# Two of the modulation's sums move from TensorE to VectorE in a two-layer diffusion backbone

## Chip, core and metric

The kernel runs on one core of one Trainium2 chip. The metric is device time in microseconds (us) of one execution. The engines are called PE (TensorE, matmuls), DVE (VectorE), ACT (ScalarE), POOL (GpSimd) and SP (SyncE); SP and POOL here issue the DMAs.

## What is computed

Two layers of a network over 256 latent tokens and 256 context tokens, 1024 wide. In each layer a modulation vector is made from the conditioning `c` (for latents) and `c_ctx` (for context), six pieces of 1024: shift, scale and gate for the mixer, then the same for the feed-forward part (FFN).

```python
mod = jax.nn.silu(c) @ w_mod[l] + b_mod[l]            # w_mod[l]: 1024 x 6144
mod_c = jax.nn.silu(c_ctx) @ w_mod[l] + b_mod[l]
sh1, sc1, g1, sh2, sc2, g2 = jnp.split(mod[:, None, :], 6, axis=-1)
shc1, scc1, gc1, shc2, scc2, gc2 = jnp.split(mod_c, 6, axis=-1)
h = rmsnorm(x, g_pre_mix[l]) * (1 + sc1) + sh1
hc = rmsnorm(xc, g_pre_mix[l]) * (1 + scc1) + shc1
y, y_ctx = token_mixer(h, hc, lp, row, col, ctx_out)   # attention, mLSTM, window attention, Fourier
x = x + g1 * rmsnorm(y, g_post_mix[l])
h2 = rmsnorm(x, g_pre_ffn[l]) * (1 + sc2) + sh2
x = x + g2 * rmsnorm(conv_ffn(h2, ...), g_post_ffn[l])
# the context stream goes the same way in the first layer
```

## The kernel before

All activations lie feature-major: 8 tiles of 128 features by 512 tokens (`KT` = 8, `T` = 512; tokens 0 to 255 are context, 256 to 511 latent; the two halves are called segments 0 and 1 below). Every large product is three matmuls (L232 to L234): weights and activations are split into a high and a low part, weights by ACT (L212) and DVE (L213), activations by ACT (`hh`) and DVE (`hl`).

The modulation is computed in rounds. `mod_rounds` takes a list of rounds, six for a layer; each round is 1024 of the 6144 outputs and reads `w_mod` in 8 pieces of 128 x 1024 (k = 0 to 7), 512 KB each. A round that is not in its argument `vector` adds up over k on PE: four matmuls for each k (L647), each with 32 columns of stationary `cs` (only two are not zero: silu of `c` and of `c_ctx`) and 256 moving columns. A round in `vector` adds up over k on DVE into two tiles of 128 x 1024, one for `c` and one for `c_ctx`: L634 for k = 0, L636 for the others, with the conditioning value as a scalar for each partition. At the end eight matmuls with a column of ones add over the partitions (L642). Both ways end with a transpose on DVE and a few small operations.

The pieces and the two sums are tiles of the pool `u`, which has 16 buffers and also holds, among much else, the four tiles of the residual stream `x` and the high and low parts of the weights loaded ahead for the FFN's first products. A round goes forward one k at a time where `between` or `fill` calls it. In layer 0 the rounds 2, 3, 4 go forward during the mixer, with loads on POOL's queue; layer 1's rounds 0, 1, 3 go forward in layer 0's `channel` (output projection, then FFN) as a filler of PE's waiting times, with loads on SP's queue.

PE's order and, in `channel`, SP's order are those of the program text (`manual_schedule`). DVE, ACT and POOL are ordered by a scheduler that works from its own costs when the program is built and takes the buffers of the pools too; on the chip each engine then keeps that order.

The place that matters besides the mixer is the closing of layer 0's projection. `closing` and `post_end` make the sums for the norm (L436 on PE, then a chain of small DVE operations), and for each of the 8 feature tiles m and each segment the residual (L522, L527), the normed tile (L401), `hh` and a full copy on ACT (L404, L408) and `hl` on DVE (L410) are made. The finished `x` tiles are written to memory by POOL (L561), two feature tiles at a time. PE's next work, the FFN's first four products, needs them m by m: first all of segment 0, then all of segment 1 (96 matmuls of 256 columns each):

```python
if j == 0:
    self.first = [[self.pf([T]) for _ in w] for w in self.ahead]
    for cs in segs:
        steps = [self.gemm_steps(p[:, cs], w, h, cs) for ps, ws in zip(self.first, self.ahead) for p, w in zip(ps, ws)]
        for _ in zip(*steps, strict=True):
            pass
```

Of the kernel before, what the change touches and what calls it, by code (L numbers as in the profile page):

```python
# [153 lines left out]
class Net:  # L154
# [1278 lines left out]
    def run(self):  # L1433
        nc = self.nc
        self.start()
        self.queue, self.fillers, self.owed, self.mods = [], [], 0, {}
        part = self.squares(self.x, slice(0, T))
        ps = self.pa([T])
        for i, p in enumerate(part):
            nc.tensor.matmul(ps, self.one, p, start=i == 0, stop=i == len(part) - 1)  # L1440
        nc.vector.tensor_scalar(self.xms, self.fold(ps, T), 1.0 / D, EPS, op0=ALU.mult, op1=ALU.add)
        rb = self.t2([T], tag="rs")
        self.unfold(self.rsqrt(self.xms), rb)
        h = self.new_h()
        A = None
        self.wtm = []
        mod, load = self.mod_rounds(0, (0, 1), nc.sync, parts=2)
        for _ in range(KT):
            load()
        after = ((), (7,), (3, 7), (3, 7, 7))  # L1450
        for q in range(4):
            self.wtm += [self.tm_weights(0, i, i >= 3) for i in ((0,), (1,), (2,), (3, 4))[q]]
            for k in range(KT):
                next(mod)
                for _ in range(after[q].count(k)):
                    next(self.tm_steps)
            ms = (2 * q, 2 * q + 2)
            A, B = self.gain(0, 1, V_GPRE, True, "A1", ms, A), self.shift(0, 0)
            for m in range(*ms):
                self.modulate(h, m, self.streams(0), rb, A, B, True)  # L1460
            if q == 0:
                self.tm_start(h, NT)
        self.start2()
        mod, load = self.mod_rounds(0, (2, 3, 4), nc.gpsimd, (3,))
        self.queue = [mod]
        for l in range(L):
            last = l == L - 1
            c0 = CTX if last else 0
            if self.dbg:
                for k in range(KT):  # L1470
                    self.dbg(f"hh{l}_{k}", h[k][0].bitcast(F32))
            if last:
                mod, load = self.mod_rounds(1, (4,), nc.gpsimd)
                self.queue = [mod]
            later, self.load = self.mod_rounds(1, (5,) if last else (0, 1, 3), nc.sync, () if last else (1, 3))
            al = self.mixer(l, h, c0)
            while self.queue:
                self.between()
            self.fillers = [later]
            if not last:  # L1480
                self.fillers.append(self.mod_rounds(0, (5,), nc.sync, (5,))[0])
            with self.tc.manual_schedule(engines={mybir.EngineType.SP}):
                h = self.channel(l, al, c0, self.load)
# [88 lines left out]
```

## Time and profile before

| | |
|---|---|
| median of three runs | 1450.48 us (1449.2 to 1450.76) |
| the profiled execution: its time, its span | 1452.06 us, 1450.3 us |
| PE busy | 1394.2 us (96%) |
| DVE busy | 957.4 us (66%) |
| ACT busy | 663.6 us (46%) |
| mean granted clock of PE | 0.987 of full |

The span runs from the first to the last instruction; 1.76 us of the execution's time lie around it. Matmuls overlap, so a matmul's own duration is longer than the step from one start to the next; costs on PE are read from starts.

### The profile page before, as it was taken

Reading aid. Unit: us, or ns where it says so; the run is one execution under the profiler, and the core shown is the slowest. Engines: PE = TensorE matmul, PEld = TensorE weight load, DVE = VectorE, ACT = ScalarE, POOL = GpSimd, SP = SyncE. Lnnn points to the kernel's source line nnn. Section 1 sums busy time; section 2 is a strip of 40 time slices with the busy share of each in tenths; the row PEclk is TensorE's granted clock in tenths of the full one; section 3 lists DMA queues with packets and bytes.
Section 4 is the critical chain, followed back from the end, with each engine's and each line's share of the span. In section 5 each row is a group of like instructions: output and inputs, shape, how many; then the busy total and the mean of one; then the engine's idle time right before and its main releaser. Section 6 shows DMA issues by size and latency. Waiting matters only on the chain.

```text
span 1450.3 us, 22235 instructions
## 1 busy us (share of the span) xinstructions
PE 1394.2 (96%) x8657; PEld 1177.2 (81%) x8657; DVE 957.4 (66%) x1955; ACT 663.6 (46%) x1156; POOL 36.3 (3%) x69
## 2 busy tenths in 40 slices
PE   6999999999999999999999999899999999899996
PEld 3887777777778889878888888687989898799996
DVE  5448687746653788853554667958676877765666
ACT  3436434324432655422332336656553655455454
POOL 0000000100000000000000000100000000000000
PEclk8999999999999999999999999999999999999998
DMA  9722232343223634343335432562333467357663
GB/s 289 272 83 92 88 132 87 131 160 102 59 73 97 206 134 168 137 160 116 116 118 163 145 117 90 202 217 88 117 115 118 136 188 244 117 174 224 184 183 94
DMA packets 73417, 208.00 MB, mean 143 GB/s; under 512 B 6880, under 2 KB 24672, under 8 KB 73184
## 3 DMA queue, kind: packets, MB, share of 16 engines
q1 hardware_dynamic: 65792, 179.32, 39.0%
q0 software_dynamic: 7520, 27.27, 5.4%
q8 instruction: 68, 1.11, 0.3%
q14 instruction: 37, 0.30, 0.1%
HBM read 201.31 MB, written 5.24 MB: 142 GB/s over the span
## 4 chain that ended last, share of the span: by engine, by line
PE 74%; DVE 8%; ACT 2%; DMA 2%; issue 1%; DVEq 0%; ACTq 0%
PE pg L232 16%; PE pg L233 15%; PE pg L234 15%; PE pa L233 7%; PE pa L232 7%; PE pa L234 7%; PE pa L787 2%; DVE wl L213 1%; PE pa L817 1%; PE pa L856 1%; PE pa L840 1%; ACT wh L212 1%; PE pa L1176 1%; PE pa L647 1%; DMA u<-wmod 1%
## 5 line engine op out<-in xcount | busy, mean ns | idle before, releaser
L213 DVE TENSOR_TENSOR wl<-st,wh 128x1024 fp32r<-128x1024 f32 (+2 forms) x262 | 313.9, 1203 | 214.9 <-ACT wh L212 213.4
L212 ACT CAST wh<-st 128x1024 fp32r<-128x1024 f32 (+2 forms) x262 | 268.8, 1032 | 370.0 <-PE pg L233 202.6
L232 PE MATMUL pg<-hh,wh 128*128 128x512 f32 (+1 forms) x1136 | 403.9, 356 | 0.7 <-DVE tg L1266 0.7
L234 PE MATMUL pg<-hh,wl 128*128 128x512 f32 (+1 forms) x1136 | 385.2, 339 | 2.3 <-DVE wl L213 2.3
L233 PE MATMUL pg<-hl,wh 128*128 128x512 f32 (+1 forms) x1136 | 384.4, 338 | 0.0
L232 PEld LDWEIGHTS pg<-hh,wh 128*128 128x128 f32 x1136 | 216.8, 191 | 31.1 <-issue 5.7
L234 PEld LDWEIGHTS pg<-hh,wl 128*128 128x128 f32 x1136 | 216.7, 191 | 26.7 <-DVE wl L213 3.1
L233 PEld LDWEIGHTS pg<-hl,wh 128*128 128x128 f32 x1136 | 216.9, 191 | 23.3 <-issue 3.1
L232 PE MATMUL pa<-hh,wh 128*128 128x256 f32 (+1 forms) x376 | 126.0, 335 | 1.4 <-ACT hh L288 1.4
L233 PE MATMUL pa<-hl,wh 128*128 128x256 f32 (+1 forms) x376 | 126.1, 335 | 0.1
L234 PE MATMUL pa<-hh,wl 128*128 128x256 f32 (+1 forms) x376 | 125.9, 335 | 0.0
L232 PE MATMUL pg<-u,wh 128*128 128x256 f32 (+1 forms) x350 | 119.8, 342 | 0.0
L233 PE MATMUL pg<-u,wh 128*128 128x256 f32 (+1 forms) x350 | 115.0, 329 | 0.0
L234 PE MATMUL pg<-u,wl 128*128 128x256 f32 (+1 forms) x350 | 114.8, 328 | 0.0
L232 PEld LDWEIGHTS pa<-hh,wh 128*128 128x128 f32 x376 | 71.4, 190 | 8.7 <-ACT hh L288 1.6
L233 PEld LDWEIGHTS pa<-hl,wh 128*128 128x128 f32 x376 | 71.4, 190 | 7.7 <-DVE hl L289 0.6
L234 PEld LDWEIGHTS pa<-hh,wl 128*128 128x128 f32 x376 | 71.4, 190 | 7.1
L232 PEld LDWEIGHTS pg<-u,wh 128*128 128x128 f32 x350 | 65.9, 188 | 12.1 <-issue 5.9
L234 PEld LDWEIGHTS pg<-u,wl 128*128 128x128 f32 x350 | 65.8, 188 | 6.6
L233 PEld LDWEIGHTS pg<-u,wh 128*128 128x128 f32 x350 | 65.9, 188 | 6.3 <-issue 0.7
L636 DVE SCALAR_TENSOR_TENSOR u<-u,cs,u 128x1024 f32<-128x1024 f32 x49 | 61.6, 1279 | 2.0 <-DMA u<-wmod 1.9
L828 ACT ACTIVATE pp<-pa,nbias 128x512 f32<-128x512 f32 (+1 forms) x48 | 29.5, 615 | 68.0 <-DVE nbias L826 37.2
(296 smaller groups left out, 2137.8 us busy)
## 6 DMA issues: line engine op xcount, KB each, us to landing
st<-wup SPq DMA_DIRECT2D x88, 512.0 KB, 3.7
st<-wgate SPq DMA_DIRECT2D x64, 512.0 KB, 3.6
u<-wmod SPq DMA_DIRECT2D x48, 512.0 KB, 4.9
u<-wmod POOLq DMA_DIRECT2D x32, 512.0 KB, 5.1
st<-wdn SPq DMA_DIRECT2D x32, 448.0 KB, 3.3
st<-win SPq DMA_DIRECT2D x26, 512.0 KB, 3.7
u<-wmod SPq DMA_DIRECT2D x32, 256.0 KB, 6.1
st<-wbr SPq DMA_DIRECT2D x16, 512.0 KB, 3.7
```

The lines of the kernel that those rows point to most:

```text
L212: nc.scalar.copy(hi[:, :cols], st[:, :cols])
L213: nc.vector.tensor_tensor(lo[:, :cols], st[:, :cols], hi.bitcast(F32)[:, :cols], op=ALU.subtract)
L232: mm(out, ah, bh, start=i == 0, stop=False)
L233: mm(out, ah, bl, start=False, stop=False)
L234: mm(out, al, bh, start=False, stop=i == n - 1)
L636: nc.vector.scalar_tensor_tensor(t, st, self.cs[:, k, i:i + 1], t, op0=ALU.mult, op1=ALU.add)
L647: nc.tensor.matmul(ps[32 * g:32 * g + 32], self.cs[:, k], st[:, g], start=k == 0, stop=k == KT - 1)
L787: ins = self.nc.tensor.matmul(O[:, j], lhs[i], rhs[i], start=i == 0, stop=i == n - 1)
L817: nc.tensor.matmul(S[:, :n], q, k, start=i == 0, stop=i == len(ops) - 1 and not m)
L828: nc.scalar.activation(P[:, :n], S[:, :n], AF.Exp, bias=nb, scale=scale, accum_out=den)
L840: nc.tensor.transpose(S[:, j * 128:j * 128 + 128], P[:, j * 128:j * 128 + 128], self.ident)
L856: ins = nc.tensor.matmul(O[64 * i:64 * i + 64, f], v_of(j, 2 * f + i), PT[i][:, j * 128:j * 128 + 128], start=j == 0, stop=j == n // 128 - 1)
```

## The change

Round 4 of layer 0 and round 0 of layer 1 are named in `vector`, so that their sums over k go to DVE.

```diff
         self.start2()
-        mod, load = self.mod_rounds(0, (2, 3, 4), nc.gpsimd, (3,))
+        mod, load = self.mod_rounds(0, (2, 3, 4), nc.gpsimd, (3, 4))
         self.queue = [mod]
...
-            later, self.load = self.mod_rounds(1, (5,) if last else (0, 1, 3), nc.sync, () if last else (1, 3))
+            later, self.load = self.mod_rounds(1, (5,) if last else (0, 1, 3), nc.sync, () if last else (0, 1, 3))
```

In the built program PE loses 64 of the four-column-group matmuls L647 and gains 16 of L642; DVE gains four L634 and 28 L636. The order of POOL and of SP keeps its kinds of instructions row by row. The names in the rows below: `u` are tiles of the pool (numbers tell them apart), `hh`, `hl` the parts of the normed activations, `t` the normed tile, `acc` the projection's output, `rs` the norm's factors.

On DVE, in the closing of layer 0's projection, segment 1, from feature tile m = 3 on, before:

```order
L401 TENSOR_TENSOR t_1094_5037<-u_4288,rs_4552 128x256
L522 TENSOR_TENSOR acc_562<-acc_562,rs_4551 128x256
L410 TENSOR_TENSOR hl_4842<-t_1093_5030,hh_4841 128x256
L527 TENSOR_TENSOR u_4290<-u_4290,acc_562 128x256
L522 TENSOR_TENSOR acc_562<-acc_562,rs_4551 128x256
L401 TENSOR_TENSOR t_1095_5045<-u_4290,rs_4552 128x256
L410 TENSOR_TENSOR hl_4844<-t_1094_5037,hh_4843 128x256
```

The same place after the change (`u_4873` and `u_4874` are the two sums, the other `u` the loaded pieces, in the order of k: 4471, 4521, 4535, 4543, 4877):

```order
L401 TENSOR_TENSOR t_1097_5018<-u_4282,rs_4546 128x256
L634 TENSOR_SCALAR u_4873<-u_4471,cs 128x1024
L410 TENSOR_TENSOR hl_4836<-t_1096_5011,hh_4835 128x256
L636 SCALAR_TENSOR_TENSOR u_4873<-u_4521,cs,u_4873 128x1024
L410 TENSOR_TENSOR hl_4838<-t_1097_5018,hh_4837 128x256
L634 TENSOR_SCALAR u_4874<-u_4471,cs 128x1024
L636 SCALAR_TENSOR_TENSOR u_4873<-u_4535,cs,u_4873 128x1024
L636 SCALAR_TENSOR_TENSOR u_4874<-u_4521,cs,u_4874 128x1024
L636 SCALAR_TENSOR_TENSOR u_4873<-u_4543,cs,u_4873 128x1024
L636 SCALAR_TENSOR_TENSOR u_4874<-u_4535,cs,u_4874 128x1024
L636 SCALAR_TENSOR_TENSOR u_4873<-u_4877,cs,u_4873 128x1024
L636 SCALAR_TENSOR_TENSOR u_4874<-u_4543,cs,u_4874 128x1024
```

Where the normed tile of m = 4 (L401 on `u_4290`) stood four rows behind that of m = 3, there now stand two L634 and twelve L636 before it; the last of them are these, with the tile of m = 4 as the last row:

```order
L636 SCALAR_TENSOR_TENSOR u_4874<-u_4887,cs,u_4874 128x1024
L522 TENSOR_TENSOR acc_562<-acc_562,rs_4545 128x256
L636 SCALAR_TENSOR_TENSOR u_4874<-u_4891,cs,u_4874 128x1024
L527 TENSOR_TENSOR u_4284<-u_4284,acc_562 128x256
L522 TENSOR_TENSOR acc_562<-acc_562,rs_4545 128x256
L401 TENSOR_TENSOR t_1098_5026<-u_4284,rs_4546 128x256
```

The sums stand there because of buffers: `u_4873` takes the buffer of the first `x` tile, which is free when POOL's write of it has landed, `u_4874` that of the second, and the pieces of k = 4, 5, 6 take those of k = 0, 1, 2.

On PE, at the start of the same closing, before, ahead of the FFN's first matmul (its last row here):

```order
L647 MATMUL pa_4879<-u_4527,cs 32x256 x4
L647 MATMUL pa_4879<-u_4541,cs 32x256 x4
L436 MATMUL pa_4886<-t_1025_4816,k 128x256
L647 MATMUL pa_4879<-u_4549,cs 32x256 x4
L436 MATMUL pa_4887<-t_1026_4817,k 128x256
L436 MATMUL pa_4888<-t_1027_4818,k 128x256
L647 MATMUL pa_4879<-u_4884,cs 32x256 x4
L647 MATMUL pa_4879<-u_4896,cs 32x256 x4
L647 MATMUL pa_4879<-u_4902,cs 32x256 x4
L232 MATMUL pg_5087<-hh_4837,u_4383 128x256
```

After the change the L436 follow each other and the FFN's first matmul comes next; the round's L642 stand behind the 192 matmuls of the FFN's first four products, where one L647 stood.

On DVE in the window attention of layer 0, after the change (`pp` are the softmax weights of one head and block, ready when L834 has scaled them):

```order
L822 TENSOR_REDUCE nm_3229<-pa_3226 128x1
L833 RECIPROCAL rec_3191<-den_3190 128x1
L636 SCALAR_TENSOR_TENSOR u_2767<-u_3179,cs,u_2767 128x1024
L834 TENSOR_SCALAR pp_3194<-pp_3194,rec_3191 128x256
L826 TENSOR_SCALAR nbias_3230<-nm_3229,nsink_3118 128x1
L636 SCALAR_TENSOR_TENSOR u_2768<-u_3179,cs,u_2768 128x1024
```

The last four of round 4's L636 stand so inside the softmax of two heads; the other twelve operations of the round stand earlier, between L213, L1266 and L1267 of the merge.

## Rows read from the trace of the kernel before

**Rows 1.** The page, part 4: the chain that ended last, share by engine.

```profile
PE 74%; DVE 8%; ACT 2%; DMA 2%; issue 1%; DVEq 0%; ACTq 0%
```

**Rows 2.** Stretches: length, then busy (x count) of PE, PEld, DVE, ACT, POOL; PEclk; DMA.

```profile
290.00:372.00 82.00, 82.00 (x414) 61.00 (x413) 45.33 (x95) 30.66 (x57) 3.17 (x6) 1.00 0.39 123
...
529.00:538.30 9.30, 7.27 (x70) 3.28 (x69) 9.30 (x37) 6.57 (x12) 0.00 (x0) 1.00 0.67 238
538.30:551.00 12.70, 12.70 (x98) 12.70 (x95) 12.70 (x52) 9.02 (x16) 1.08 (x2) 0.87 0.50 199
...
562.80:660.00 97.20, 97.20 (x442) 78.90 (x442) 66.01 (x77) 35.21 (x46) 0.00 (x0) 1.00 0.45 152
```

**Rows 3.** Timeline of PE in layer 0's mixer: start, us, instruction.

```profile
302.07 0.39 PE L233 MATMUL pg<-hl,wh 128*128 128x512 f32 x1
302.30 0.39 PE L234 MATMUL pg<-hh,wl 128*128 128x512 f32 x1
302.62 0.64 PE L647 MATMUL pa<-u,cs 128*32 128x256 f32 x8
303.18 0.51 PE L232 MATMUL pg<-u,wh 128*128 128x512 f32 x1
303.53 0.39 PE L233 MATMUL pg<-u,wh 128*128 128x512 f32 x1
```

**Rows 4.** Timeline of PE where round 3 adds over partitions.

```profile
281.45 1.07 PE L642 MATMUL pa<-u,col 128*32 128x256 f32 x16
282.45 0.51 PE L232 MATMUL pg<-u,wh 128*128 128x512 f32 x1
```

**Rows 5.** DVE's instructions of L634 and L636: ns min/median/max.

```profile
L634 DVE TENSOR_SCALAR u<-u,cs x7: 747/748/752, 182.8 to 754.4; 128x1024 f32<-128x1024 f32 x7
...
L636 DVE SCALAR_TENSOR_TENSOR u<-u,cs,u x49: 1273/1279/1285, 188.5 to 848.5; 128x1024 f32<-128x1024 f32 x49
```

**Rows 6.** Timeline of DVE: two L636 in a row, and the closing of the projection.

```profile
534.24 0.43 DVE L410 TENSOR_TENSOR hl<-t,hh 128x256 fp32r<-128x256 f32 x1
...
547.18 0.76 DVE L527 TENSOR_TENSOR u<-u,acc 128x256 f32<-128x256 f32 x2
...
548.86 0.42 DVE L401 TENSOR_TENSOR t<-u,rs 128x256 f32<-128x256 f32 x1
...
554.34 1.22 DVE L213 TENSOR_TENSOR wl<-st,wh 128x1024 fp32r<-128x1024 f32 x1
...
557.53 0.43 DVE L410 TENSOR_TENSOR hl<-t,hh 128x256 fp32r<-128x256 f32 x1 [0.17 <-ACT t L408]
...
578.23 2.48 DVE L636 SCALAR_TENSOR_TENSOR u<-u,cs,u 128x1024 f32<-128x1024 f32 x2
```

**Rows 7.** Timeline of PE: first matmul of the FFN's first products, later ones, the end.

```profile
538.26 0.52 PE L232 MATMUL pg<-hh,u 128*128 128x256 f32 x1
...
541.57 0.38 PE L232 MATMUL pa<-hh,u 128*128 128x256 f32 x1
...
562.63 0.28 PE L234 MATMUL pa<-hh,u 128*128 128x256 f32 x1
562.84 0.64 PE L647 MATMUL pa<-u,cs 128*32 128x256 f32 x8
```

**Rows 8.** Timeline of ACT in the closing.

```profile
556.26 0.60 ACT L404 ACTIVATE hh<-t,mod,A 128x256 fp32r<-128x256 f32 x1 [1.24 <-DVE t L401]
```

**Rows 9.** Timeline of POOL: writes of the first and second `x` tile.

```profile
545.89 0.54 POOL L561 DMA_DIRECT2D xd<-u  x1 [218.82 <-DVE u L527]
548.24 0.54 POOL L561 DMA_DIRECT2D xd<-u  x1 [1.81 <-DVE u L527]
```

**Rows 10.** Issue to landing: POOL's writes of `x`, then SP's loads of `wmod` (529 to 563).

```profile
DMA to landing us min/median/max: 2.9/3.7/5.0
...
DMA to landing us min/median/max: 3.6/4.8/6.4
```

**Rows 11.** Timelines of DVE and PE in the window attention.

```profile
355.84 0.43 DVE L822 TENSOR_REDUCE nm<-pa 128x1 f32<-128x256 f32 x1
...
357.92 0.38 PE L840 MATMUL pa<-k,pp 128*128 128x128 f32 x2
```

## Prediction

> **What bounds the kernel now.** I read the chain of waits first: three quarters of it are PE, DVE has 8% [rows 1]. So a microsecond taken off PE is worth a microsecond only where PE never waits, and one put on DVE costs nothing only where nobody waits for DVE. I looked at the two places of the change with the busy times by stretch. In layer 0's mixer, where round 4 runs, PE is busy 82.0 of 82.0 us and DVE 45.33 [rows 2]: work taken off PE counts, and DVE has room. In the closing of layer 0's projection, where layer 1's round 0 runs, it is the other way about: from 529.0 to 551.0 DVE is busy 22.0 of 22.0 us [rows 2], while PE's sequence of matmuls has holes (weight loads 3.28 of 9.30 us in the first part). There the round's matmuls fill PE's time while it waits for the normed activations, which DVE makes. After 562.8 PE is busy without a gap for at least 97 us [rows 2], so a delay of PE at 562.8 is made up nowhere near.
>
> **Round 4 of layer 0.** Eight times four L647 go. In the stream of 512-column matmuls, from L234 (302.30) to the second matmul behind (303.53) it takes 1.23 us; two steps of 0.23 us (302.07 to 302.30) would take 0.46 [rows 3]. So one k costs 0.77 us, eight cost 6.2. Added are eight L642; round 3's took 1.00 us from their start to the next matmul's [rows 4], and with the same 0.2 us around them as L647 (0.77 less the 0.56 from 302.62 to 303.18 [rows 3]) 1.2. PE gains 5.0 us, and it counts, since PE has no wait there.
>
> DVE gets 2 L634 of 0.75 us and 14 L636 of 1.28 [rows 5], 19.4 us, where it has 36.7 us free [rows 2]. Twelve of the sixteen stand between the weight splits and the merge's updates, whose tiles PE takes up later; I cost them at nothing, the cover being the idle half of DVE, and without it their 14 us would stand on the path at most once. The last four stand in softmaxes. One head's chain is tight: its reciprocal now follows the maximum of the next head (done at 355.84 + 0.43 = 356.27), then come one L636 (1.2) and two short operations of about 0.5 together, so its weights are ready at about 358.0, and PE wanted them at 357.92 [rows 11], some tenths earlier still with the L647 before it gone. I take 0.3 us, bounds 0 and 2.4 (two L636 in full). Sum of this place: -4.7.
>
> **Round 0 of layer 1: what goes.** Seven groups of L647 leave the closing. That alone would help: the FFN's first matmul started at 538.26 [rows 7], though the first `hl` was ready at 534.24 + 0.43 = 534.67 [rows 6]. It would start 3.6 us earlier. But this only gains if the last matmul of those products comes earlier, and that one waits for the last `hl`.
>
> **What comes, and who waits for it.** By the listing DVE's operations up to L401 of m = 3, segment 1, are the same as before; that one ends by 549.2 [rows 6]. The first L634 needs the buffer of the first `x` tile, written out by POOL from 545.89 [rows 9], landing 3.7 us later [rows 10]: 549.6. From there to L401 of m = 4 stand 2 L634 (a step of 0.67: the 0.75 less the overlap of 0.08 that two L636 in 2.48 us show), 12 L636 (2.48 - 1.28 = 1.20 a step), and six operations of 256 columns, L401 among them (0.76 - 0.42 = 0.34 a step [rows 5, 6]): 1.3 + 14.4 + 2.0 = 17.7 us, so L401 of m = 4 ends at 567.3.
>
> Do the loads hold it up more? The load of k = 4 needs the buffer of k = 0, free after the second L634 at 552.8; it lands 4.8 us later [rows 10], at 557.6, just when DVE comes to it (552.8 + 4 x 1.2 = 557.6). k = 5 and 6 follow two L636 (2.4 us) apart each, as DVE does. At 6.4 us, the longest of these landings, the run would end 1.6 later, once.
>
> From L401 of m = 4 to `hl` of m = 7 DVE has 12 operations of 256 columns, two L213 (1.22 less the overlap: 1.14 each [rows 6]) and two L636: 4.1 + 2.3 + 2.4 = 8.8 us, so the last `hl` is done at 576.1. ACT's two operations for a tile (0.6 us each [rows 8]) fit between. Before, it was done at 557.53 + 0.43 = 558.0 [rows 6]. Behind it PE has eleven matmuls. Their step is 0.12 us: from 541.57 to 562.84 there are 176 [rows 7]. So the products end at 576.1 + 1.3 = 577.4, where they ended at 562.63 + 0.12 = 562.75 [rows 7]: 14.7 us later. PE has nothing else in its order meanwhile; the products of m = 0 to 3 are through by about 554 (`hl` of m = 3 is done at 552.1, and its twelve matmuls take 1.4 us), so that DVE's run stands bare for some 13 us.
>
> **The clock.** [...] PE will now wait longer, and again before m = 7. I add 1.4 for the restart, bounds 0 and 2.8 (twice). [...]
>
> **Behind the products** eight L642 take the place of the one L647 group that stood there: 1.00 less 0.56 [rows 3, 4], 0.4 more. POOL's later writes of `x` and the loads that take their buffers move with the products, and the FFN's next weights with them; I cost that at nothing, since the weights for the next three products are loaded already; without that cover it would be a load's landing, 4.8 us [rows 10].
>
> **Sum:** -5.0 + 0.3 + 14.7 + 1.4 + 0.4 = +11.8 us. The profiled execution took 1452.06 us, so it would be 1463.9; the median of the runs is 1.58 lower, 1450.48, and I predict 1462.3 for it. Bounds: without the clock term and the softmax term, and with the write landing at 2.9 us (DVE goes on at 549.2), 9.7: 1460.2. With the write at 5.0 (+1.3), loads at 6.4 (+1.6), the clock twice (+1.4) and the softmaxes at 2.4 (+2.1), 18.2: 1468.7. A difference under 0.2% (2.9 us) could hardly be told from none here.
>
> **Rivals.** (1) The stall reaches the end only in part: the cost of the closing is right, but somewhere in the FFN or layer 1 a wait of before shrinks because PE comes later. For it: PE's chain share is 74, not 100%. Against: no wait of PE for 97 us behind the place [rows 2]. One such wait of 4.8 us, a load's landing [rows 10], falling away whole gives 1457.5.
> (2) Faster: DVE's sums stay off the path, if the normed tiles of segment 1 did not queue behind them. Then PE keeps the 5.0 us, and the products start 3.6 us earlier and, at one step, end so: 1450.48 - 8.6 = 1441.9. It decides where the sums end before 551 or stand behind the last `hl`; the listing says neither, and DVE is full to 551.0. [...]
> (3) No change: the delay on DVE is about a third of what I count, 5 us instead of 14.7. This needs L636 at a rate that no row has (it would be 0.4 us). 1450 to 1453.
> (4) Worse: the wait for buffers goes round. Loads on SP stand in order, so a load that waits for a late `x` write holds up the FFN's weights behind it. One landing (4.8) more: 1467.1, two 1471.9. For it: the last writes of `x` now come some 14 us later. Against: the products come as much later.
>
> **How the numbers follow.** Likeliest 0.66 (1459.5 to 1468.7); rival 1 0.12 (1453.5 to 1459.5); rival 2 0.05; rival 3 0.05; rival 4 beyond 1468.7 0.12. The range 1457.0 to 1469.0 leaves out rivals 2 and 3, part of 1 and most of 4, about 2 in 10. Faster by over 0.2%: rival 2, 0.05. Within: rival 3, 0.05. Slower: the rest, 0.90.
>
> **What would show it.** In the changed profile: PE idle for some 13 us, released by DVE's `hl` or ACT's `hh`, in segment 1's products; twelve L636 and two L634 on DVE ahead of it, the first ending a wait on the write of `x`; DVE's last `hl` there some 18 us later against the last sums L436 than before; the lower clock once PE goes on. In the mixer: the stream shorter by about 5 us with no new wait over a microsecond in the window attention. I am wrong if PE shows no such hole, if later waits shrink by several microseconds, or if weights come late behind it.

## The result and the profile after

| | before | after |
|---|---|---|
| median of the runs of the first comparison | 1450.62 us (4 runs, 1449.2 to 1451.27) | 1464.8 us (4 runs, 1461.46 to 1465.7) |
| the profiled execution: its time, its span | 1452.06 us, 1450.3 us | 1465.7 us, 1463.9 us |
| mean granted clock of PE | 0.987 | 0.979 |

The change makes the kernel slower: the ratio is 1.0101, with an interval of 1.0083 to 1.0118, and the difference of the medians 14.2 us. A second comparison gave 1462.36 us against 1450.98, ratio 1.008 (1.006 to 1.0101).

I read the waits of PE first. Over the whole run of the kernel after, the longest (columns: who waits for whom, us in total, times, longest):

```profile
PE pg L232 <- ACT hh L404: 17.6, 3, 13.5
...
PE pa L647 <- DMA u<-wmod: 8.5, 18, 1.6
PE pg L233 <- DVE hl L410: 4.5, 5, 1.6
...
PE pa L840 <- DVE pp L834: 2.7, 1, 2.7
```

One wait of 13.5 us for `hh` is new. The wait for the softmax (L840) is as long in the kernel before (2.7 us) and stands in layer 1; in layer 0's window attention no wait came up. The stretches of the closing show where the hole is, answering to [rows 2] (length, then busy of PE, PEld, DVE, ACT, POOL; PEclk; DMA):

```profile
290.00:376.00 86.00, 86.00 (x410) 68.48 (x409) 66.16 (x125) 31.42 (x61) 4.23 (x8) 1.00 0.44 142
524.00:533.30 9.30, 7.86 (x51) 6.45 (x49) 9.30 (x36) 5.85 (x12) 0.00 (x0) 1.00 0.00 1
533.30:546.00 12.70, 11.99 (x89) 11.84 (x89) 12.70 (x59) 8.59 (x16) 0.54 (x1) 0.87 0.01 1
546.00:580.00 34.00, 18.23 (x131) 16.23 (x130) 32.36 (x52) 11.06 (x19) 1.60 (x3) 0.80 0.60 204
580.00:680.00 100.00, 100.00 (x448) 81.24 (x447) 63.62 (x73) 35.31 (x47) 0.00 (x0) 1.00 0.44 146
```

In the mixer (first row) PE is still busy throughout. From 546 to 580 it is busy 18.23 of 34 us, while DVE is busy 32.36. What DVE does there (timeline: start, us, instruction, idle time before and who ended it):

```profile
533.68 0.42 DVE L410 TENSOR_TENSOR hl<-t,hh 128x256 fp32r<-128x256 f32 x1
...
548.28 0.45 DVE L401 TENSOR_TENSOR t<-u,rs 128x256 f32<-128x256 f32 x1
548.62 0.78 DVE L634 TENSOR_SCALAR u<-u,cs 128x1024 f32<-128x1024 f32 x1
...
551.50 0.75 DVE L634 TENSOR_SCALAR u<-u,cs 128x1024 f32<-128x1024 f32 x1 [0.23 <-DMA xd<-u]
552.17 12.04 DVE L636 SCALAR_TENSOR_TENSOR u<-u,cs,u 128x1024 f32<-128x1024 f32 x10
...
566.33 0.42 DVE L401 TENSOR_TENSOR t<-u,rs 128x256 f32<-128x256 f32 x1
...
575.07 0.42 DVE L410 TENSOR_TENSOR hl<-t,hh 128x256 fp32r<-128x256 f32 x1
```

The first L401 is that of m = 3, the second that of m = 4; between them stand the sums, as the listing had it. On PE the hole ends with the `hh` of m = 4:

```profile
533.07 0.38 PE L232 MATMUL pg<-hh,u 128*128 128x256 f32 x1 [0.84 <-ACT hh L404]
...
567.44 0.58 PE L232 MATMUL pg<-hh,u 128*128 128x256 f32 x1 [13.55 <-ACT hh L404]
568.53 0.58 PE L233 MATMUL pg<-hl,u 128*128 128x256 f32 x1 [0.51 <-DVE hl L410]
568.91 0.41 PE L234 MATMUL pg<-hh,u 128*128 128x256 f32 x1
...
572.32 0.31 PE L232 MATMUL pg<-hh,u 128*128 128x256 f32 x1
...
575.54 0.38 PE L233 MATMUL pg<-hl,u 128*128 128x256 f32 x1 [0.80 <-DVE hl L410]
...
576.81 0.28 PE L234 MATMUL pa<-hh,u 128*128 128x256 f32 x1
577.02 1.07 PE L642 MATMUL pa<-u,col 128*32 128x256 f32 x16
578.02 0.50 PE L232 MATMUL pg<-hh,wh 128*128 128x512 f32 x1
```

The chain of waits is no help for a comparison here, and it is worth seeing why. Its share by engine after, against [rows 1], and three of its pieces (start, us, what):

```profile
PE 56%; issue 18%; DVE 9%; ACT 2%; DMA 2%; POOL 0%; DVEq 0%; ACTq 0%; POOLq 0%
```

```profile
328.85 216.47 issue
...
547.69 3.79 DMA xd<-u
...
553.36 2.47 DVE u L636 x2
```

It runs back from the sums to the landing of POOL's write of the second `x` tile, which ended the wait of 0.23 us, and then along POOL, which had stood idle for 216 us. One wait of 0.2 us thus turned 15% of the span into "issue". PE did not lose 18 points of its time (it is busy 95% of the span, 96% before); the path was drawn elsewhere.

**Stage by stage.** Some instructions stand in every version, so that the profiles can be laid side by side: the first L642 on PE (round 3 of layer 0, [rows 4]), the first and the last `hl` (L410) of the closing [rows 6], the first 512-column matmul behind the FFN's first four products (563.41 before, 578.02 above), and the first L436 of the FFN's norm. All lengths in us, from the profiled execution; the versions in the lower rows are those of the experiments below.

| version | start to L642 | to first `hl` (holds round 4) | first to last `hl` | to 512 columns | to L436 (FFN) | rest |
|---|---|---|---|---|---|---|
| before | 281.4 | 252.8 | 23.3 | 5.9 | 337.8 | 549.1 |
| after | 285.5 | 248.2 | 41.4 | 2.9 | 338.0 | 547.9 |
| after, again | 282.1 | 248.3 | 41.4 | 3.0 | 338.0 | 548.0 |
| r4_only | 281.7 | 248.0 | 23.3 | 5.5 | 337.7 | 547.4 |
| r4_again | 282.6 | 248.0 | 23.3 | 3.6 | 337.7 | 546.2 |
| r0_only | 280.9 | 252.8 | 41.0 | 3.0 | 337.8 | 547.9 |
| one_sum | 282.4 | 248.1 | 32.8 | 2.5 | 337.3 | 546.7 |
| room2 | 281.1 | 254.4 | 26.6 | 3.0 | 337.3 | 547.0 |
| late | 282.2 | 248.2 | 23.3 | 2.4 | 346.9 | 548.6 |
| late2 | 281.4 | 248.1 | 23.3 | 2.4 | 348.8 | 546.6 |
| late3 | 281.7 | 247.9 | 23.3 | 2.4 | 346.6 | 548.9 |
| late4 | 285.9 | 248.1 | 23.3 | 2.4 | 343.5 | 549.1 |

Between the two profiled executions of the first comparison the span grew by 13.6 us: the start +4.1, the stage with round 4 -4.6, the closing +18.1 and -3.0, the FFN +0.2, the rest -1.2. Two entries were in no forecast: the start and the rest.

### The profile page after: what moved, and what is told of

The parts are those of the page before. It is cut to its first block, busy times and chain, and to the rows that moved or that the text cites. A ratio compares the mean times of both kernels' runs of the same rounds, so it can differ in the third digit from the quotient of the medians.

```text
span 1463.9 us, 22071 instructions
## 1 busy us (share of the span) xinstructions
PE 1390.3 (95%) x8561; PEld 1178.4 (80%) x8561; DVE 992.1 (68%) x1987; ACT 663.0 (45%) x1156; POOL 36.3 (2%) x69
## 4 chain that ended last, share of the span: by engine, by line
PE 56%; issue 18%; DVE 9%; ACT 2%; DMA 2%; POOL 0%; DVEq 0%; ACTq 0%; POOLq 0%
PE pg L232 11%; PE pg L233 10%; PE pg L234 10%; PE pa L232 6%; PE pa L233 6%; PE pa L234 6%; PE pa L787 2%; DVE wl L213 1%; DVE u L636 1%; ACT wh L212 1%; PE pa L1176 1%; PE pa L856 1%; DMA st<-wup 1%; DMA st<-wgate 1%; PE pa L817 1%
## 5 line engine op out<-in xcount | busy, mean ns | idle before, releaser
L213 DVE TENSOR_TENSOR wl<-st,wh 128x1024 fp32r<-128x1024 f32 (+2 forms) x262 | 313.9, 1203 | 197.2 <-ACT wh L212 195.8
L212 ACT CAST wh<-st 128x1024 fp32r<-128x1024 f32 (+2 forms) x262 | 268.8, 1032 | 369.8 <-PE pg L233 195.1
L234 PE MATMUL pg<-hh,wl 128*128 128x512 f32 (+1 forms) x1136 | 385.2, 339 | 1.3 <-DVE wl L213 1.2
L234 PEld LDWEIGHTS pg<-hh,wl 128*128 128x128 f32 x1136 | 216.2, 190 | 26.6 <-DVE wl L213 2.9
L234 PE MATMUL pa<-hh,wl 128*128 128x256 f32 (+1 forms) x376 | 126.0, 335 | 0.0
L234 PE MATMUL pg<-u,wl 128*128 128x256 f32 (+1 forms) x350 | 115.3, 329 | 0.0
L636 DVE SCALAR_TENSOR_TENSOR u<-u,cs,u 128x1024 f32<-128x1024 f32 x77 | 96.4, 1282 | 2.2 <-DMA u<-wmod 2.1
L234 PEld LDWEIGHTS pa<-hh,wl 128*128 128x128 f32 x376 | 71.4, 190 | 7.1
L234 PEld LDWEIGHTS pg<-u,wl 128*128 128x128 f32 x350 | 66.0, 189 | 6.5
```

The costliest lines, as they stand in the source:

```text
L212: nc.scalar.copy(hi[:, :cols], st[:, :cols])
L213: nc.vector.tensor_tensor(lo[:, :cols], st[:, :cols], hi.bitcast(F32)[:, :cols], op=ALU.subtract)
L234: mm(out, al, bh, start=False, stop=i == n - 1)
L636: nc.vector.scalar_tensor_tensor(t, st, self.cs[:, k, i:i + 1], t, op0=ALU.mult, op1=ALU.add)
```

## The experiments

The theory (A): the two parts are independent and add up; round 4 gains 4.7 us because PE sets the pace in the mixer, round 0 costs 15 us because DVE sets it in the closing; the longer start varies from execution to execution. Rival B: the start belongs to the changed program. Rivals C to G are named where they were put to the test.

**r4_only** leaves round 0 on PE, **r0_only** leaves round 4 there, and the changed kernel ran again beside them (**after, again** in the table). The first two edits are shown against the kernel before.

```diff
-        mod, load = self.mod_rounds(0, (2, 3, 4), nc.gpsimd, (3,))
+        mod, load = self.mod_rounds(0, (2, 3, 4), nc.gpsimd, (3, 4))
```

> Only round 4 of layer 0 goes to VectorE; layer 1's round 0 stays on TensorE. Theory A (the two parts add up; the first 70 us, 3.8 us longer in the profile after the change, vary from execution to execution and are none of the change's): 4.7 us faster than before, 1445.9, with the gain between 287 and 382 us and nothing in the closing. Rival B (those 3.8 us belong to the changed program): the gain is mostly eaten up at the start, 1449.5 to 1450. Rival D (freeing TensorE in the mixer gains nothing, something else sets its pace): 1450.6.

Measured: 1445.24 us against 1450.98, ratio 0.9963 (0.995 to 0.9977), and again in a later comparison (**r4_again**, below) 1443.27 against 1449.81, 0.9964 (0.995 to 0.9979). In r4_only's row of the table the stage with round 4 differs clearly, by 4.8 us; the rest, 1.7 shorter, comes up again below. In r4_again's row two later stages are shorter too, by 2.3 and 2.9 us; its program is r4_only's, so these are differences between executions. Theory A has the 4.8; rivals B and D fall.

```diff
-            ... self.mod_rounds(1, (5,) if last else (0, 1, 3), nc.sync, () if last else (1, 3))
+            ... self.mod_rounds(1, (5,) if last else (0, 1, 3), nc.sync, () if last else (0, 1, 3))
```

> Only layer 1's round 0 goes to VectorE; round 4 of layer 0 stays on TensorE. Theory A: all of the loss is in the closing of layer 0's projection, 15.2 us from its first sums to the fourth product's end and the matmuls behind; with a change of up to 1.5 us in layer 1 either way this gives 1464 to 1467. Rival B: 3.8 more, 1468 to 1470. Rival C (the closing is late for another reason than VectorE's sums, such as round 4's timing): near 1450.

Measured: 1466.33 us, ratio 1.0107 (1.0089 to 1.0126). First to last `hl` takes 41.0 us instead of 23.3, nothing before it has moved, and the loss is all in the closing: 44.0 us from the first `hl` to the 512-column matmul instead of 29.2. Theory A; rival C falls.

> The changed kernel once more. Theory A: the start takes what before's took in one execution or another, so the times spread over about 4 us below 1465.7, and a profile with the short start has some 1461 to 1462; the closing's delay is again 15.2 us and round 4's gain 4.8. Rival B: every execution has the long start, times 1464 to 1466, and the profile's first 75 us are again 3 to 4 us behind those of before.

Measured: 1462.36 us (1460.77 to 1464.89). The start took 282.1 us, 0.7 more than before's, with the same program as in the execution that took 285.5; every other stage agrees with that one to 0.1 us. The three starts together (281.7, 280.9, 282.1) speak against rival B.

The long start came up early, where no instruction of the change has come yet. The same L410 on DVE starts at 24.83 us before and at 23.65 after, a later L410 at 50.46 and 52.83, an L1022 at 67.01 and 70.80; from there on the distance stays at 3.8 to 4.1. So 2.4 us of it are there by 50 us. What happens between 50 and 72 us, the first row before, the second after:

```profile
50.00:72.00 22.00, 18.92 (x125) 18.08 (x124) 7.49 (x24) 9.74 (x16) 0.00 (x0) 0.92 0.62 228
```

```profile
50.00:72.00 22.00, 17.82 (x108) 17.09 (x107) 9.12 (x26) 10.37 (x17) 0.00 (x0) 0.84 0.70 267
```

Weights came later (DMA share 0.70 instead of 0.62 in this stretch, a wait of 3.5 instead of 2.2 us for a split), and PE's clock was 0.84 on the mean instead of 0.92. What made an execution's start long is not shown.

**late** keeps both rounds on DVE but moves layer 1's rounds out of the closing altogether (its edit is against the changed kernel).

```diff
+        held, self.fillers = self.fillers, [] if not last else self.fillers
         self.project(l, al, c0, G, load)
...
         next(self.ws)
+        self.fillers = held
         self.ffn(l, h, c0, not last)
...
                 self.ffn_up(l, h, j, g[-1], segs)
-                self.fill(0.5)
+                self.fill(0.75 if more else 0.5)
```

> Both rounds on VectorE, but none of layer 1's rounds goes forward in the closing: they start with the FFN's first product, one and a half steps instead of one to a product so that they are through in time. Theory A: TensorE's hole of 13 us goes, VectorE's last low part there comes as early as before, the fourth product ends 3.4 to 5 us earlier against the closing's first sums, round 4's 4.7 us stay, eight more L642 cost 1: 1441 to 1443. Rival E (VectorE's 19 us merely go elsewhere: in the FFN they make TensorE wait as long): 1452 to 1460. Rival B: 1445 to 1447.

Measured: 1451.4 us, ratio 0.9999 (0.9988 to 1.0011). My number was wrong by 9 us, half of the theory right: the hole is gone (first to last `hl` 23.3, as before), and PE is at the 512 columns 2.4 us behind the last `hl` instead of 5.9. Of these 3.5 us, 0.65 are the L647 group that stood behind the products. The L647 ahead of the products let them start 4.0 us after the first `hl` began, where they now start 0.6 before it, but at full clock that costs little: in r4_again, with the L647 in their old places, PE needed only 3.6 us. There the 12.7 us from the products' first matmul on have a clock of 1.00, where before has 0.87 [rows 2] and r4_only, at 5.5 us, 0.87 too:

```profile
534.30:547.00 12.70, 12.70 (x112) 12.69 (x109) 12.70 (x53) 8.90 (x16) 1.07 (x2) 1.00 0.52 204
```

So some 2 of the 3.5 us go with the lower clock that this execution of before happened to have. Late's first products had a lower clock too (the mean from 520 to 580 was 0.97), but behind them PE still waited 0.90 us for an `hl` (at 544.80), so the loss lay under DVE's time.

But the FFN takes 9.1 us longer. That is rival E's mechanism at about half of its price; 1451.4 lies just below its range. PE, then ACT, then DVE at the place:

```profile
573.61 0.50 PE L234 MATMUL pa<-hh,wl 128*128 128x512 f32 x1 [0.62 <-DVE wl L213]
...
581.37 0.51 PE L232 MATMUL pg<-hh,wh 128*128 128x512 f32 x1 [2.44 <-ACT wh L212]
...
583.84 0.79 PE L234 MATMUL pg<-hh,wl 128*128 128x512 f32 x1 [1.73 <-DVE wl L213]
```

```profile
571.32 0.63 ACT L1356 ACTIVATE pp<-pp 128x512 f32<-128x512 f32 x1 [7.22 <-DVE pp L1011]
...
579.75 0.63 ACT L1356 ACTIVATE pp<-pp 128x512 f32<-128x512 f32 x1 [4.95 <-DVE pp L1011]
580.29 1.03 ACT L212 CAST wh<-st 128x1024 fp32r<-128x1024 f32 x1
```

```profile
574.07 1.28 DVE L636 SCALAR_TENSOR_TENSOR u<-u,cs,u 128x1024 f32<-128x1024 f32 x1
...
575.86 1.28 DVE L636 SCALAR_TENSOR_TENSOR u<-u,cs,u 128x1024 f32<-128x1024 f32 x1
...
577.72 1.28 DVE L636 SCALAR_TENSOR_TENSOR u<-u,cs,u 128x1024 f32<-128x1024 f32 x1
578.91 0.75 DVE L1011 SCALAR_TENSOR_TENSOR pp<-pg,vec,pp 128x510 f32<-128x510 f32 x1
```

The sums stand on DVE ahead of L1011, ACT waits for L1011 and has the split L212 behind it in its own order, and PE waits for the split. A stall of DVE reaches PE here by way of another engine's queue. From 573 to 597 PE's clock was 0.86 on the mean.

**late2** and **late3** are late with fillers that start later, so that the first weights are split before.

```diff
-                self.fill(0.75 if more else 0.5)
+                self.fill((0 if j < 4 else 1) if more else 0.5)
```

(late3, against late; late2 has `0 if j < 2 else 0.5 if j < 4 else 0.75`.)

> As the experiment before (both rounds on VectorE, no filler in the closing), but the fillers start only with the FFN's fifth product, then two steps to a product. Theory A (in the experiment before, the gain of 8.5 us at the first product was lost between 572 and 596 us, where round 0's sums stood on VectorE ahead of the weight splits L213 and the FFN's activations of the first products, and TensorE's clock fell behind the wait): without them there the loss goes, 1442 to 1445. Rival F (VectorE is too full in the FFN wherever the sums stand): 1449 to 1453, with waits for L213 later.

> As the last, but the fillers start with the FFN's third product, at one step for two products and then one and a half. Theory A: between the two, 1443 to 1449, since the first sums still come while the first weights are split. Rival F: 1449 to 1453.

Measured: late3 1451.77 us, ratio 1.0001 (0.9986 to 1.0016); late2 1454.09, 1.0024 (1.0011 to 1.0037). Both expectations of theory A missed. In late3 the place from 573 to 597 was cured, and PE had one wait in the whole FFN:

```profile
820.77 2.28 PE L642 MATMUL pa<-u,col 128*32 128x256 f32 x16 [3.93 <-DVE u L636]
```

The L642 of a round follow its last sum at once in PE's order, and DVE was behind. With the slower steps after the wait (matmuls at 0.43 instead of 0.23 us; the clock from 820 to 900 was 0.96 on the mean) it cost some 7 us of the 8.9: from the last matmul ahead of the wait to the end of the slow ones it took 10.9 us, where the steps and the L642 at full clock make 3.7. In late2 the FFN took 11.0 us longer, with a wait of 1.9 us for a split (L213) and two of 4.0 together for the last sums.

**late4** is late3 with two steps between a round's last sum and its L642.

```diff
-                        yield 1
+                        yield 1 if l == 0 and r < 5 else 2400
```

> As the version whose fillers start with the FFN's fifth product at two steps each, but two steps lie between a round's last sum and its eight L642 on TensorE. In that version the 6.6 us kept after the closing were lost at one place, 816.5 to 828 us, where the L642 of the last round stood in TensorE's order before VectorE had its last sums (a wait of 3.9 us, and the lower clock behind it). Theory A (VectorE has room in the FFN; only the order at single places costs): the wait goes and 1443 to 1445.5 is left. Rival F (VectorE is too full in the FFN, so that the wait comes elsewhere): 1448 to 1452.

> Only round 4 of layer 0 on VectorE, once more beside the experiment on the same chip: 1444.5 to 1446, as before. If the other is faster than this one, layer 1's round 0 on VectorE is worth having once it is kept out of the closing; if not, round 4 alone is the best version.

Measured: late4 1448.79 us, ratio 0.9995 (0.9983 to 1.0008); r4_again 1443.27, a little below its 1444.5 to 1446. That wait went, and others came (columns as above):

```profile
PE pg L234 <- DVE wl L213: 3.2, 2, 1.9
```

The FFN still takes 5.7 us longer than before; 1.2 of it are round 0's eight L642 [rows 4] and 3.2 these two waits. For the remaining 1.3 I have no row. Rival F holds in this sense: in four tries at the order and spacing, the 18 us of sums in the FFN made PE wait somewhere. Whether a spacing exists that doesn't is left open. r4_only is the best version of the study.

**one_sum** halves the disputed work. The context's sum of layer 1's round 0 is left out.

```diff
-                        sums = [self.u([4, 256]) for _ in range(2 if l < L - 1 or r < 2 else 1)]
+                        sums = [self.u([4, 256]) for _ in range(2 if l < L - 1 or r == 1 else 1)]
```

> The changed kernel with one sum less in layer 1's round 0: the context's shift of the mixer is left out (its sum over k, seven operations in the closing and one behind it). Theory A: the run of sums between the normed tiles of m = 3 and 7 is one L634 and six L636, some 7.9 us instead of 15.1, so the closing's delay falls from 15.4 to 7 or 8 us: 1452 to 1455. Rival C (the delay is a wait for a write or a load, however many sums stand there): as the changed kernel, 1460 to 1463.

Measured: 1453.55 us, ratio 1.0019 (1.0004 to 1.0034), as theory A has it. First to last `hl` is 32.8 us, 9.5 above before. One L634 and six L636 are 0.67 + 6 x 1.20 = 7.9, and DVE waited once for a piece, which the longer run of sums had hidden:

```profile
554.57 1.28 DVE L636 SCALAR_TENSOR_TENSOR u<-u,cs,u 128x1024 f32<-128x1024 f32 x1 [1.93 <-DMA u<-wmod]
```

7.9 + 1.9 = 9.8. Rival C has the 1.9 us for itself here; for the rest it falls a second time: the price goes with the number of sums.

**room2** loads two pieces ahead instead of four, so that two buffers are free for the sums.

```diff
-        room = 4 if c0 == 0 else 6
+        room = 2 if c0 == 0 else 6
```

> The changed kernel, but SP loads two pieces of round 0 ahead in the projection instead of four. Two of the pool's buffers are then free for the sums at once, and by the listing five of the sixteen operations stand before the norm's first sums, nine inside segment 0's norm and its normed tiles, and none between the normed tiles of segment 1. Theory A (the buffers set the place, and the price is VectorE's time in the closing's chain): the hole of 13 us in segment 1's products goes; segment 0's normed tiles come up to 11 us later and TensorE waits there instead, less what it has to wait anyway: 1450 to 1457. Rival G (any place in the closing costs the same, the 16 operations in full): 1460 to 1464.

Measured: 1453.52 us, ratio 1.0022 (1.0009 to 1.0035). The buffers do set the place: the run of sums left segment 1, and the hole with it. What came instead is a wait in front of the norm,

```profile
527.97 5.52 PE L436 MATMUL pa<-t,k 128*128 128x256 f32 x12 [3.94 <-DVE t L429]
```

so that the stage to the first `hl` is 6.2 us longer than after's 248.2, and first to last `hl` 3.3 longer than before. Up to the last `hl` 9.5 us of the 18.1 remain on the path; that the others lie beside PE's work in the projection is my reading. Rival G falls: the price depends on the place.

## Why the prediction was right

The forecast was 1462.3 us (1457 to 1469); the two comparisons gave 1464.8 and 1462.4. Step by step:

- **Round 4, -5.0.** The stage shrank by 4.6 (after), 4.5 (again) and 4.8 (r4_only and r4_again). PE has no wait of its own in 290 to 376, before or after, so the costing from starts of matmuls held to some tenths.
- **Softmax, +0.3.** No wait of PE came up in the window attention, in after or in r4_only. Round 4's L642 took 1.01 us to the next matmul's start (380.42 to 381.43 in after), as round 3's did. What the 0.2 to 0.5 missing from the 5.0 are is not shown; with the softmax the forecast had 4.7.
- **DVE's run.** L401 of m = 4 was to end at 567.3 on the clock of before; it ended at 566.33 + 0.42 = 566.75 after, where everything in the closing stood 0.56 earlier (533.68 against 534.24 [rows 6]), so 567.3. First to last `hl` grew by 18.1, as worked out. One detail was off: not the first L634 waited for a write, but the second, 0.23 us for the second tile's.
- **The products' end, +14.7.** From the first `hl` to the last L234 it was 562.63 - 534.24 = 28.4 and became 576.81 - 533.68 = 43.1: 14.7. It is 18.1 less some 3.4, because before's products ended 5.1 us behind the last `hl` and after's 1.7. That distance before is partly the clock of this one execution: in r4_again, whose closing is the same program, the products ended 26.1 us behind the first `hl`, and against that the term would be some 17. The forecast took before's end from the same execution that it was compared with, so this agreement to a tenth is in part luck.
- **The clock, +1.4: wrong.** The 1.4 for the restart was my estimate, and no run shows it as a term of the change. In its place the runs showed this: PE did go on slower, with a clock of 0.50 from 568.9 to 572.3 and 0.80 over 546 to 580; the 16 steps from 568.91 to 572.32 are 0.213 us each, where later ones are 0.12. But the slow matmuls belong to m = 4 and 5, and PE then waited again, 0.80 us, for `hl` of m = 7. They ran under the wait, so the term is 0. I had added a slow restart to a path that DVE was setting. In before's closing PE set the end, and there the lower clock counted (0.51 from 538.3 to 541.5): from 538.26 to 541.57 [rows 7] fifteen steps took 3.31 us, where fifteen of 0.12 make 1.8, a loss of 1.5. r4_again did without it and was through 2.3 us sooner, 0.4 of it by an earlier first matmul.
- **Behind the products, +0.4.** From the last L234 to the next matmul 1.21 us instead of 0.78: 0.43.
- **Rivals.** (1) asked for a wait that shrinks in the FFN or in layer 1. The FFN took 0.2 longer. The rest got 1.2 shorter, but so it did where nothing was delayed (r4_only 1.7, r4_again 2.9): before's profile had a stretch of lower clock there that after's had not.

```profile
1195.60:1200.60 5.00, 3.94 (x18) 3.76 (x19) 4.17 (x7) 2.14 (x4) 0.00 (x0) 0.66 0.79 224
```

```profile
1210.50:1213.90 3.40, 2.62 (x19) 2.42 (x20) 3.21 (x5) 1.79 (x3) 0.00 (x0) 1.00 0.74 200
```

  (before, and the same matmuls after: 0.66 against 1.00.) So it isn't the change's. (2), with the sums off the path, is what the late versions built: of its 8.6 us 8.1 came in at the products' end (4.6 + 3.5 in late) and were given back in the FFN, which the rival had not priced. (3) and (4) did not show; no weight came late behind the hole.

The terms that held make -4.6 + 14.7 + 0.4 = +10.5. Against it stand +14.2 and +11.4 in the two comparisons, and the two parts alone, -5.74 and +15.35, make +9.6. In the profiled execution of after the gap is its start, 4.1 us longer; whether the other runs of that comparison had it is not shown. The forecast had nothing for the start and 1.4 us too much for the clock, and that wrong term brought its +11.8 nearer to both medians: luck.

## What to carry to other kernels

Ask at each place which engine the stage waits for, not what an engine's busy share is over the run: the same move from PE to DVE gained 4.7 us in a stage that PE paced and lost 15 in one that DVE paced, and both came out of counting operations by their step. In a queue that keeps its order, what a long operation costs is set by what stands behind it, on its own engine and on the engines that wait in turn (18.1 us more on DVE from first to last `hl` moved the products' end on PE by 14.7); freeing its place only pays if the new place has nobody waiting (four arrangements of round 0's sums in the FFN were tried here, and none was free). A slow restart cost only where PE, not its supplier, set the end: nothing after the change (clock 0.50 from 568.9 to 572.3), some 2 us in before's closing (0.51 from 538.3 to 541.5). A term that agrees to a tenth with one profile should be held against a second profile of the same program.

## What the runs showed of the hardware

- The same program up to the first L642 took from 280.9 to 285.9 us in the twelve profiles; two of them (after, late4) lie about 4 us above the others. The 436 instructions of DVE and the 251 of ACT up to there are the same, in the same order, before and after. Executions of one kernel spread from 1441.65 to 1447.94 us for r4_only and from 1446.09 to 1455.52 for before, so a difference of 3 us needs many runs here.
- On DVE the steps add up to some tenths: 14 L636 and two L634 at steps of 1.20 and 0.67 make 18.1 us, and a whole closing grew by 18.1 in after and by 17.7 in r0_only.
- A wait of PE of 3.9 us (late3) was followed by the sixteen L642 in 2.28 instead of 1.07 us and nine matmuls at 0.43 instead of 0.23 us a step; the waits of 1.3 and 1.9 us in late4 left no such mark in the mean clock of their stretches (1.00). In late, after waits of 2.4 and 1.7 us shortly one behind the other, the mean clock from 573 to 597 was 0.86, and the L234 behind the second wait (583.84) took 0.79 us instead of 0.39.
- One program ran the same matmuls at two different mean clocks: over the 12.7 us from the FFN's first matmul on the mean clock was 0.87 in r4_only, as in before [rows 2], whose closing is the same, and 1.00 in r4_again. The first sixteen steps took 3.42 and 1.97 us.
